# Forget logits in fp32 in the quarters of a bank, and the first bias rows loaded over ScalarE's queue, in a streaming encoder kernel

## The chip, the cores and the metric

The kernel runs on one core of a Trainium2 chip. The time is that of one execution on the device, in microseconds (us). Matrix products run on TensorE (PE in the profile, its weight loads PEld), elementwise work on VectorE (DVE), ScalarE (ACT) and GpSimd (POOL); SyncE (SP) issues DMA transfers, and so can ScalarE and GpSimd, each over a queue of its own.

## The reference

Two layers run over 640 tokens of width 1024: 512 of a prompt and 8 x 16 new ones of samples. Layer 0 mixes with a chunked gMLP. Layer 1, in which the change lies, is forgetting attention with 16 heads of 128 channels. With h the normalized input of the layer:

```
proj = h @ w_in                                  # q, k, v, z (2048 columns each), then 16 forget logits
logf = log_sigmoid(proj[..., 4 * E:] + b_f)      # one number per token and head
cT = cumsum(logf)                                # along the tokens, for each head
s = q @ k.T * dh ** -0.5 + cT[query] - cT[key]   # later keys masked
y = softmax(s) @ v * silu(z), then @ w_out
```

The samples attend in the same way to 256 cached rows and their own new ones. `logf` of all tokens is an output too.

## The kernel before, in words

**Data.** h stands transposed in the tile A as two halves h_hi and h_lo whose sum is h (type fp32r, 8 k-tiles of 128 channels by 640 tokens). A product in full precision is made of several fp32r matmuls over such halves: L272, L273 and L274 are the three of a product. Weights come as units of 512 KB by DMA into RAW or R (for the attention layer GpSimd issues them, L122), GpSimd forms sums of blocks (L211, into sff), and ScalarE (L289) and VectorE (L290) split each unit into two fp32r halves in W. Most projections are made as seven block products in place of eight. For these, `right_operands` (L570) needs the four quarters of whole h, in fp32: (i, j) is half i of the channels by half j of the tokens (320 each). Three were copied by ScalarE when h was made (KEPT, L323); the fourth, (1, 0), is joined from the halves by one VectorE addition, L578.

**Order.** The source lists the work of the projections as steps (`interleave`, L370), and pieces of other work with due times in us are called between the steps. A scheduler that simulates the engines then fixes the order on each engine; every engine works its list in order. `behind` and `queued` pin a piece behind a given instruction.

**The stage.** The attention layer begins with `project_v0` (L1032; matmuls L1040 and L1041), then `project_k0` and `project_q`/`project_z`. Between the steps of `project_v0` stand:

- `forget_logits` (L955): the forget weights, 128 x 8 x 16, are split into two fp32r halves side by side in WF (L932). In two token ranges, 0 to 384 and 384 to 640 (SPLITS), 16 matmuls each (L961, L962, L964) bring w_hi and w_lo times h_hi, and w_hi times h_lo, into 32 and 16 rows of a bank. ScalarE copies them out (L965).
- `log_forget` (L967): five transposes of 32 x 128 (L970), a copy and two additions on VectorE, then log_sigmoid.
- `forget_sums` (L987): the cumulative sums as matmuls with a triangle of ones (L990 for the prompt, L998 to L1000 for the samples). ScalarE copies the results out (L991, L1001) and stores them by DMA: c_sc (16 heads x 512) and cs_sc (the samples' rows, mask of the later scores).

From there on each head needs its bias rows back, spread over 128 partitions: `load_w0(h)` loads row h of c_sc (256 KB; into a slot of sff for even heads, into CST for odd ones), and `load_mask(i)` loads rows of cs_sc (136 KB). For head 0, head 1 and the first mask GpSimd issues these loads (L122, a helper line that names the queue); later ones are issued by ScalarE. VectorE turns a row into the bias of a query block (L1141), and ends the scores of a block with L1151 or L1154, before ScalarE's exponential (L1157) and the normalization (L1162). For the samples it adds a mask to the last 16 columns (L1222), and four matmuls side by side, each writing 32 rows of a bank, make the scores (L1225). L709, L720, L722 and L725 take the block products of the projections out of the banks; L1096 and L1104 are ScalarE's parts of q and z; L317 are transposes of the projections.

## Time and profile before

| | |
|---|---|
| time, median of 3 runs (lowest, highest) | 1284.0 us (1283.24, 1284.87) |
| the profiled execution | 1284.04 us |
| its span | 1281.7 us |
| mean granted TensorE clock | 0.998 |
| busy share: PE, PEld, DVE, ACT, POOL | 99%, 89%, 75%, 46%, 28% |
| chain that ended last: PE, DVE, DMA, issue | 94%, 3%, 2%, 1% |

The span runs from the first to the last instruction. The busy share is that of the whole span, so an engine with 75% can still be the late one in a single stage. A row of a timeline gives start, duration, engine, line, operation, output<-input, shapes and count; where the engine stood idle before it, the brackets give for how long and which engine's result, or which transfer, ended it. A row "PE ... <- DVE ..." of the waits gives the total time that TensorE stood until VectorE's instruction, how often, and the longest. Instructions overlap in the pipeline of TensorE, so what a matmul costs is read from the distance of two starts.

### The profile page before, as it was taken

How to read it: one execution, taken by the hardware profiler on the slowest of the kernel's cores; microseconds unless marked ns; L12 is line 12 of the kernel's file. 1: busy time of each engine (PE TensorE's matmuls, PEld its weight loads, DVE VectorE, ACT ScalarE, POOL GpSimd, SP SyncE). 2: the span in 40 equal slices, each digit the busy share in tenths (PEclk: the TensorE clock that was granted, in tenths of full speed). 3: DMA queues.
4: the chain of work that ended last, by engine and by line, in shares of the span. 5: the costliest groups of instructions: out<-in, count | busy, mean ns of one | idle time of the engine just before them, and what ended most of it. 6: DMA issues, size and time to landing. Idle time of an engine off the chain costs nothing.

```text
span 1281.7 us, 21124 instructions
## 1 busy us (share of the span) xinstructions
PE 1270.6 (99%) x7881; PEld 1141.4 (89%) x7881; DVE 955.7 (75%) x1796; ACT 594.9 (46%) x1075; POOL 360.3 (28%) x326
## 2 busy tenths in 40 slices
PE   9999999999999999998999999999999999999998
PEld 7888999999988888887999999999999999788887
DVE  6844999999944374797987898989897988545643
ACT  5424555444535253554544454545444445445331
POOL 1012444453000010245334545454434430000100
PEclk9999999999999999999999999999999999999999
DMA  5532344232324213548887767677888759632211
GB/s 201 179 99 66 114 122 126 85 98 88 120 95 152 82 50 99 139 105 152 166 168 164 188 162 173 147 179 146 147 160 189 178 106 267 247 128 83 67 62 54
DMA packets 275360, 171.52 MB, mean 134 GB/s; under 512 B 188761, under 2 KB 238601, under 8 KB 275258
## 3 DMA queue, kind: packets, MB, share of 16 engines
q1 hardware_dynamic: 261170, 127.80, 36.5%
q0 software_dynamic: 10000, 36.71, 13.9%
q10 hardware_dynamic: 4088, 5.67, 1.5%
q8 instruction: 62, 1.02, 0.3%
q14 instruction: 40, 0.33, 0.1%
HBM read 148.55 MB, written 21.59 MB: 133 GB/s over the span
## 4 chain that ended last, share of the span: by engine, by line
PE 94%; DVE 3%; DMA 2%; issue 1%; SPq 0%; ACT 0%; POOL 0%; ACTq 0%; DVEq 0%; POOLq 0%
PE pb L272 26%; PE pb L273 26%; PE pb L274 26%; PE pb L1175 3%; PE pb L419 2%; PE pb L1252 2%; PE pb L1168 1%; PE pb L1225 1%; PE pb L317 1%; PE pb L741 1%; DMA out<-R 1%; DVE W L290 1%; PE pb L1040 1%; PE pb L1053 1%; PE pb L1249 1%
## 5 line engine op out<-in xcount | busy, mean ns | idle before, releaser
L272 PE MATMUL pb<-A,W 128*128 128x320 f32 (+1 forms) x752 | 241.4, 321 | 1.9 <-DVE R L720 1.6
L273 PE MATMUL pb<-A,W 128*128 128x320 f32 (+1 forms) x752 | 234.4, 312 | 0.0
L274 PE MATMUL pb<-A,W 128*128 128x320 f32 (+1 forms) x752 | 233.9, 311 | 0.0
L290 DVE TENSOR_TENSOR W<-RAW,W 128x1024 fp32r<-128x1024 f32 (+1 forms) x122 | 148.2, 1215 | 72.5 <-ACT W L289 70.5
L273 PE MATMUL pb<-W,A 128*128 128x512 f32 x498 | 194.6, 391 | 0.0
L272 PE MATMUL pb<-W,A 128*128 128x512 f32 x498 | 194.5, 393 | 0.0
L274 PE MATMUL pb<-W,A 128*128 128x512 f32 x498 | 193.8, 392 | 0.0
L289 ACT ACTIVATE W<-RAW 128x1024 fp32r<-128x1024 f32 (+1 forms) x122 | 115.8, 949 | 91.1 <-PE pb L274 43.4
L272 PEld LDWEIGHTS pb<-A,W 128*128 128x128 f32 x752 | 142.0, 189 | 3.0 <-DVE R L720 1.8
L273 PEld LDWEIGHTS pb<-A,W 128*128 128x128 f32 x752 | 142.1, 189 | 0.6 <-issue 0.2
L274 PEld LDWEIGHTS pb<-A,W 128*128 128x128 f32 x752 | 141.8, 189 | 0.0
L272 PE MATMUL pb<-tbf,W 128*128 128x320 f32 x360 | 118.9, 330 | 0.0
L303 POOL TENSOR_TENSOR SML<-SML 128x1 f32<-128x1 f32 x20 | 14.9, 748 | 351.2 <-DVE SML L301 346.5
L274 PE MATMUL pb<-tbf,W 128*128 128x320 f32 x360 | 111.4, 309 | 0.0
L273 PE MATMUL pb<-tbf,W 128*128 128x320 f32 x360 | 111.2, 309 | 0.0
L274 PEld LDWEIGHTS pb<-W,A 128*128 128x128 f32 x498 | 93.4, 188 | 19.5 <-issue 0.4
L273 PEld LDWEIGHTS pb<-W,A 128*128 128x128 f32 x498 | 93.6, 188 | 18.7
L272 PEld LDWEIGHTS pb<-W,A 128*128 128x128 f32 x498 | 93.5, 188 | 18.6
L211 POOL TENSOR_TENSOR sff<-RAW 128x512 f32<-128x512 f32 x46 | 59.4, 1292 | 178.8 <-DVE W L290 107.6
L709 DVE TENSOR_TENSOR R<-R,pb 128x320 f32<-128x320 f32 x184 | 86.3, 477 | 15.3 <-PE pb L274 13.6
L290 DVE TENSOR_TENSOR A<-R,A 128x640 fp32r<-128x640 f32 (+1 forms) x42 | 34.4, 853 | 56.6 <-ACT A L289 56.2
L272 PEld LDWEIGHTS pb<-tbf,W 128*128 128x128 f32 x360 | 67.7, 188 | 9.8 <-issue 6.2
(280 smaller groups left out, 2860.7 us busy)
## 6 DMA issues: line engine op xcount, KB each, us to landing
RAW<-in_fox_w_in POOLq DMA_DIRECT2D x46, 512.0 KB, 7.4
RAW<-in_gmlp_w_in SPq DMA_DIRECT2D x40, 512.0 KB
R<-in_cache_fox_k SPq DMA_DIRECT2D x128, 128.0 KB
R<-in_cache_fox_v SPq DMA_DIRECT2D x32, 512.0 KB
RAW<-in_gmlp_w_out SPq DMA_DIRECT2D x16, 512.0 KB
RAW<-in_ple_w_gate SPq DMA_DIRECT2D x16, 512.0 KB
RAW<-in_fox_w_out SPq DMA_DIRECT2D x16, 512.0 KB
R<-in_fox_w_in POOLq DMA_DIRECT2D x14, 512.0 KB, 8.1
```

Of the source, the lines that this page charges most:

```text
L211: nc.gpsimd.tensor_tensor(out=o, in0=a, in1=b, op=op)
L272: nc.tensor.matmul(out, lh, rh, start=start, stop=False)
L273: nc.tensor.matmul(out, lh, rl, start=False, stop=False)
L274: nc.tensor.matmul(out, ll, rh, start=False, stop=stop)
L289: first = nc.scalar.activation(out=hi, in_=src, func=AF.Copy)
L290: nc.vector.tensor_tensor(out=lo, in0=src, in1=f(hi), op=ALU.subtract)
L303: behind["pool"] = nc.gpsimd.tensor_tensor(out=q, in0=t, in1=mhalf, op=ALU.pow)
L317: behind["pe"] = nc.tensor.transpose(out=b[:, j * P:(j + 1) * P], in_=src[:, (4 * c + j) * P:(4 * c + j + 1) * P], identity=ident)
L419: line[e] = make(*args, **kw)
L709: behind["dve"] = nc.vector.tensor_tensor(out=into(i, j), in0=a, in1=b, op=ALU.add)
L1175: nc.tensor.matmul(O[:, d], v[:, j, hh * P:(hh + 1) * P], pt[:, j * P:(j + 1) * P], start=(j == 0), stop=(j == i))
L1252: nc.tensor.matmul(O[32 * bl:32 * bl + 32, :256], pt[:, t * P + 32 * bl:t * P + 32 * bl + 32], vv[:, bl, t], start=False, stop=(t == 1))
```

## The change

The forget logits are formed from whole h in fp32. WF becomes fp32 and holds the raw forget weights twice, so that a matmul brings 32 rows of which 16 count twice over. Tokens 0 to 511, four tiles of 128, go into the four quarters (32 rows each) of one bank; tile 2 lies across the two halves of the tokens and takes two matmuls of 64 columns per k-tile. The samples' tile goes into a second bank, with two k-tiles in each quarter, and the four partial sums are added later by one reduction on VectorE. That makes 48 matmuls, two copies on ScalarE and two 128 x 128 transposes. The quarter (1, 0) of h is joined ahead of `project_v0`, since the logits now read it, and `right_operands` takes it as ready. The due times of the pieces in `project_v0` change.

The loads of the rows of heads 0 and 1 and of the first mask are issued by ScalarE, the first of them pinned behind the store of cs_sc.

The diff; new line numbers are some 4 to 18 higher than the old ones (L1141 is L1159 in the new file, L1222 is L1240, L1040 is L1058, L964 and its like become L968):

```diff
@@ -68,7 +68,7 @@
     psum = tc.alloc_tile_pool(name="psum", bufs=1, space=PSUM)
     dram = tc.alloc_tile_pool(name="dram", bufs=1, space=DRAM)
     W = sbuf.tile([P, NW * 2048], F32R, name="W")
-    WF = sbuf.tile([P, 256], F32R, name="WF")
+    WF = sbuf.tile([P, 256], F32, name="WF")
     A = sbuf.tile([P, 10240], F32R, name="A")
     RAW = sbuf.tile([P, NRAW * 1024], F32, name="RAW")
     CST = sbuf.tile([P, C_N], F32, name="CST")
@@ -564,6 +564,11 @@
     def quarter(i, j):
         return tuple(z[:, 4 * i:4 * i + 4, j * HT:(j + 1) * HT] for z in (h_hi, h_lo))
 
+    def joined_quarter(o, i, j):
+        q = r1(o, 1280).rearrange("p (k n) -> p k n", k=4)
+        hi, lo = quarter(i, j)
+        nc.vector.tensor_tensor(out=q, in0=f(hi), in1=f(lo), op=ALU.add)
+
     def right_sum(i):
         return tuple(TB[:, z:z + 4 * HT].rearrange("p (k n) -> p k n", k=4) for z in (i * 2560, i * 2560 + 1280))
 
@@ -574,8 +579,7 @@
         last = t_a if ready else b12
         for q, (i, j) in zip((b11, b12, b21, b22), ((0, 0), (0, 1), (1, 0), (1, 1))):
             if (i, j) not in ready:
-                hi, lo = quarter(i, j)
-                nc.vector.tensor_tensor(out=q, in0=f(hi), in1=f(lo), op=ALU.add)
+                joined_quarter(at[2 * i + j], i, j)
         for o, a, b, dst in ((t_a, b12, b11, 0), (t_b, b22, t_a, 1), (b21, b21, t_b, 2), (last, b22, b12, None)):
             nc.vector.tensor_tensor(out=o, in0=a, in1=b, op=ALU.subtract)
             if dst is not None:
@@ -932,7 +936,8 @@
     wf_raw = tmpa(128).rearrange("p (k n) -> p k n", k=8)
     dma(wf_raw, f_win[0, :, 4 * E:].rearrange("(k p) n -> p k n", p=P))
     wf = WF.rearrange("p (k n) -> p k n", k=8)
-    split(wf[:, :, :H], wf[:, :, H:], wf_raw)
+    for z in (0, H):
+        nc.scalar.activation(out=wf[:, :, z:z + H], in_=wf_raw, func=AF.Copy)
     bfb = tmpa(H)
     dma(bfb, b_f[0].partition_broadcast(P))
     cc = tmpa(256).rearrange("p (t b h) -> p t b h", t=2, b=NB)
@@ -943,8 +948,7 @@
     for t in range(2):
         nc.vector.tensor_copy(out=cr[:, t].rearrange("p (r b h) -> p r b h", r=NB, b=NB), in_=cc[:, t].rearrange("p b (r h) -> p r b h", h=2))
 
-    fT = tmpa(TOK, 32)
-    ft = tmpa(NT * 32).rearrange("p (t c h) -> p t c h", t=NT, c=2)
+    fT = tmpa(2 * P)
     n = NT * H
     fx, fa, fe, fl, fu, lft = (r1(o_V + 1280 + z * n, n) for z in range(6))
     lf3 = lft.rearrange("p (t h) -> p t h", t=NT)
@@ -952,25 +956,37 @@
     cT, ex, cS = r1(o_PT + 288, SEQ, H), r1(o_PT + 800, P), r1(o_V + 1760, 272)
     assert o <= o_K and o_PT + 288 >= o_P + 1280 and o_PTs + 96 >= o_qp + 1280
 
+    def whole(i, j):
+        return r1(KEPT[i, j], 1280).rearrange("p (k n) -> p k n", k=4)
+
     def forget_logits():
-        for (a, b) in SPLITS:
-            pb = bank(ATT)
-            for k in range(8):
-                hi, lo = h_at(k, a, b)
-                if k == 0:
-                    nc.tensor.matmul(pb[:32, :b - a], wf[:, k], hi, start=True, stop=False)
-                nc.tensor.matmul(pb[:H, :b - a], wf[:, k, :H], lo, start=False, stop=False)
-                if k > 0:
-                    nc.tensor.matmul(pb[:32, :b - a], wf[:, k], hi, start=False, stop=(k == 7))
-            nc.scalar.activation(out=fT[:, a:b], in_=pb[:32, :b - a], func=AF.Copy)
+
+        pb = bank(ATT), bank(ATT)
+
+        def add(g, z, t, k, start, stop, j):
+            a, b = max(t * P, j * HT), min((t + 1) * P, (j + 1) * HT)
+            nc.tensor.matmul(pb[z][32 * g:32 * g + 32, a - t * P:b - t * P], wf[:, k], whole(k // 4, j)[:, k % 4, a - j * HT:b - j * HT],
+                             start=start, stop=stop)
+
+        for k in range(8):
+            for t, j in ((0, 0), (1, 0), (3, 1)):
+                add(t, 0, t, k, k == 0, k == 7, j)
+            for n in (2 * k, 2 * k + 1):
+                add(2, 0, 2, n % 8, n % 8 == 0, n % 8 == 7, n // 8)
+        for z in range(2):
+            for g in range(4):
+                add(g, 1, 4, 2 * g + z, z == 0, z == 1, 1)
+        for z in range(2):
+            nc.scalar.activation(out=fT[:, z * P:(z + 1) * P], in_=pb[z][:, :P], func=AF.Copy)
 
     def log_forget():
         pb = bank(ATT)
-        for t in range(NT):
-            nc.tensor.transpose(out=pb[:, t * 32:(t + 1) * 32], in_=fT[:, t * P:(t + 1) * P], identity=ident[:32, :32])
-        nc.vector.tensor_copy(out=ft, in_=pb[:, :NT * 32].rearrange("p (t c h) -> p t c h", t=NT, c=2))
-        nc.vector.tensor_tensor(out=fx3, in0=ft[:, :, 0], in1=ft[:, :, 1], op=ALU.add)
-        nc.vector.tensor_tensor(out=fx3, in0=fx3, in1=bfb.unsqueeze(1).broadcast_to([P, NT, H]), op=ALU.add)
+        for z in (0, P):
+            nc.tensor.transpose(out=pb[:, z:z + P], in_=fT[:, z:z + P], identity=ident)
+        groups = pb[:, :2 * P].rearrange("p (z g h) -> p z g h", z=2, h=32)[:, :, :, :H]
+        nc.vector.tensor_tensor(out=fx3[:, :4], in0=groups[:, 0], in1=bfb.unsqueeze(1).broadcast_to([P, 4, H]), op=ALU.add)
+        nc.vector.tensor_reduce(out=fx3[:, 4], in_=groups[:, 1].rearrange("p g h -> p h g"), op=ALU.add, axis=mybir.AxisListType.X)
+        nc.vector.tensor_tensor(out=fx3[:, 4], in0=fx3[:, 4], in1=bfb, op=ALU.add)
 
         nc.vector.scalar_tensor_tensor(out=fa, in0=fx, scalar=-1.0, in1=fx, op0=ALU.mult, op1=ALU.max)
         nc.scalar.activation(out=fe, in_=fa, func=AF.Exp, scale=-1.0)
@@ -999,7 +1015,9 @@
         nc.tensor.matmul(pb[:, P:272], cr[:, 1], tri[:, :272 - P], start=False, stop=False)
         nc.tensor.matmul(pb[:, 256:272], ex, CST[:, C_T16:C_T16 + TS], start=False, stop=True)
         nc.scalar.activation(out=cS, in_=pb[:, :272], func=AF.Copy)
-        dma(cs_sc, cS, nc.scalar)
+        behind["act"] = nc.scalar.dma_start(out=cs_sc, in_=cS)
+        with queued("act"):
+            load_w0(0, nc.scalar)
 
 
     def v_of(p):
@@ -1323,15 +1341,17 @@
     sums = []
 
     def sums_of_h():
-        sums.append(right_operands((KEPT[0, 0], KEPT[0, 1], o_qp, KEPT[1, 1], o_P), KEPT))
+        sums.append(right_operands((KEPT[0, 0], KEPT[0, 1], KEPT[1, 0], KEPT[1, 1], o_P), KEPT))
 
     def first_k():
         with queued("sp"):
             load_k(0, 0, 0)
 
-    interleave(project_v0(), [(0.0, forget_logits), (2.0, log_forget), (2.1, sums_of_h), (9.0, forget_sums),
-                              (9.1, lambda: load_w0(0, nc.gpsimd)), (1.0, first_k)])
-    interleave(project_k0(), [(11.0, lambda: turn_k(0, 0, 0)), (11.1, lambda: load_k(0, 0, 1)), (0.0, lambda: load_w0(1, nc.gpsimd)), (0.1, lambda: load_mask(0, nc.gpsimd)), (6.0, lambda: load_v(0, 0))])
+    KEPT[1, 0] = o_qp
+    joined_quarter(o_qp, 1, 0)
+    interleave(project_v0(), [(3.0, forget_logits), (4.5, log_forget), (4.6, sums_of_h), (9.0, forget_sums),
+                              (1.0, first_k)])
+    interleave(project_k0(), [(11.0, lambda: turn_k(0, 0, 0)), (11.1, lambda: load_k(0, 0, 1)), (3.0, lambda: load_mask(0, nc.scalar)), (3.1, lambda: load_w0(1, nc.scalar)), (6.0, lambda: load_v(0, 0))])
     split(*quarter(0, 1), sums[0])
     nc.gpsimd.memset(r1(o_qp, 512), 0.0)
     interleave(project_q(0), [(8.0, lambda: turn_k(0, 0, 1)),
```

How the order moves. First TensorE in `project_v0`: pb_70 to pb_73 are the banks of the v projection, pb_74 that of the logits, R_69 the large working tile. This stands on TensorE in the middle of the v projection before:

```order
L1040 MATMUL pb_71<-W,A 128x512
L1041 MATMUL pb_71<-W,A 128x256
L1040 MATMUL pb_71<-W,A 128x512
L317 MATMUL pb_75<-CST,R_69 128x128 x4
L962 MATMUL pb_74<-A,WF 16x384 x2
L964 MATMUL pb_74<-A,WF 32x384
L962 MATMUL pb_74<-A,WF 16x384
L317 MATMUL pb_76<-CST,R_69 128x128 x4
L964 MATMUL pb_74<-A,WF 32x384
```

And this stands on TensorE now, where the large piece of the logits begins, late in the v projection:

```order
L1058 MATMUL pb_73<-W,A 128x512
L968 MATMUL pb_74<-R_69,WF 32x128
L968 MATMUL pb_74<-R_69,WF 32x64 x2
L968 MATMUL pb_74<-R_69,WF 32x128 x3
L968 MATMUL pb_74<-R_69,WF 32x64 x2
L968 MATMUL pb_74<-R_69,WF 32x128 x3
L968 MATMUL pb_74<-R_69,WF 32x64
L317 MATMUL pb_77<-CST,R_69 128x128 x4
L317 MATMUL pb_75<-CST,R_69 128x128 x4
L968 MATMUL pb_74<-R_69,WF 32x64
```

On what moved: part of the old logits lay one or two at a time between other matmuls, the rest in runs; the new ones, each of 64 or 128 columns, stand in four pieces of 2, 13, 25 and 8 matmuls.

Then ScalarE at the end of the cumulative sums: rows with DMA are transfers that it issues. The order on ScalarE before:

```order
L289 ACTIVATE W<-RAW 128x512
L718 ACTIVATE R_69<-pb_71 128x320
L991 ACTIVATE R_69<-pb_74 16x512
L122 DMA c_sc<-R_69 16x512
L289 ACTIVATE W<-sff 128x1024
L1001 ACTIVATE R_69<-pb_75 128x272
L122 DMA cs_sc<-R_69 128x272
```

The order on ScalarE now, at the same place:

```order
L289 ACTIVATE W<-RAW 128x512
L722 ACTIVATE R_69<-pb_71 128x320
L1007 ACTIVATE R_69<-pb_74 16x512
L1017 ACTIVATE R_69<-pb_75 128x272
L122 DMA c_sc<-R_69 16x512
L1018 DMA cs_sc<-R_69 128x272
L289 ACTIVATE W<-sff 128x1024
L122 DMA sff<-c_sc 128x512
L122 DMA CST<-c_sc 128x512
L122 DMA R_69<-cs_sc 128x1x272
```

The three loads of bias rows now stand between the two stores and the next work of ScalarE (L1096, now L1114), with one weight split between the stores and the loads.

And GpSimd at the same place, where these loads stood. The order on GpSimd before:

```order
L122 DMA RAW<-in_fox_w_in 128x4x256 x2
L1205 COPY R_69<-R_69 128x4x16
L122 DMA sff<-c_sc 128x512
L122 DMA CST<-c_sc 128x512
L211 TENSOR_TENSOR sff<-RAW 128x512
L122 DMA R_69<-cs_sc 128x1x272
L211 TENSOR_TENSOR sff<-RAW 128x512
L211 TENSOR_TENSOR sff<-sff,RAW 128x512
L211 TENSOR_TENSOR sff<-RAW,sff 128x512
```

The order on GpSimd now:

```order
L122 DMA RAW<-in_fox_w_in 128x4x256 x2
L1223 COPY R_69<-R_69 128x4x16
L211 TENSOR_TENSOR sff<-RAW 128x512 x2
L211 TENSOR_TENSOR sff<-sff,RAW 128x512
L211 TENSOR_TENSOR sff<-RAW,sff 128x512
L122 DMA RAW<-in_fox_w_in 128x4x256
```

GpSimd keeps its weight loads and sums (L211), without the three loads between them.

## The prediction

> **What bounds the kernel now.** I read the page first, then the waits of TensorE, then the timelines of the engines named there, and last the clock and the DMA share by windows.
>
> ```profile
> span 1281.7 us, 21124 instructions
> ...
> PE 1270.6 (99%) x7881; PEld 1141.4 (89%) x7881; DVE 955.7 (75%) x1796; ACT 594.9 (46%) x1075; POOL 360.3 (28%) x326
> ```
>
> TensorE is busy for 99% of the span. So a change pays in two ways only: TensorE gets less to do, or one of its few stands goes. Of its waits, these three are the ones behind the stage that the change touches:
>
> ```profile
> PE pb L272 <- DVE SML L1154: 2.0, 1, 2.0
> PE pb L272 <- DVE R L720: 1.6, 1, 1.6
> PE pb L272 <- DVE R L725: 0.3, 1, 0.3
> ```
>
> All name VectorE. Its timeline shows why it was late (start, duration, engine, line, operation, and in brackets the idle time before it with its releaser):
>
> ```profile
> 587.06 0.61 DVE L1141 TENSOR_TENSOR R<-sff,CST 128x128 f32<-128x128 f32 x1 [5.64 <-DMA sff<-c_sc]
> 587.60 2.92 DVE L290 TENSOR_TENSOR W<-R,W 128x512 fp32r<-128x512 f32 x2
> 590.44 1.76 DVE L290 TENSOR_TENSOR W<-RAW,W 128x512 fp32r<-128x512 f32 x1
> 592.12 0.47 DVE L720 TENSOR_TENSOR R<-R,pb 128x320 f32<-128x320 f32 x1
> ```
>
> VectorE, which works in order, stood from 581.42 to 587.06 us for the bias rows of head 0. Behind them were queued three weight splits (4.6 us), and behind those L720, whose result TensorE stood 1.6 us for. The stand of 2.0 us at L1154 is ten us later in the same backlog. Then comes the clock (columns: window; its length; busy time and count of PE, PEld, DVE, ACT, POOL; granted clock; DMA share; GB/s):
>
> ```profile
> 572.50:575.50 3.00, 3.00 (x23) 3.00 (x22) 3.00 (x6) 1.35 (x2) 2.92 (x3) 1.00 0.05 11
> 603.80:607.20 3.40, 3.40 (x16) 3.40 (x15) 3.40 (x3) 0.89 (x3) 3.32 (x3) 0.50 0.24 37
> ```
>
> Right behind the stands the clock is granted at 0.50 for 3.4 us: at half speed TensorE loses 1.7 us there. At stake in this place are 2.0 + 1.6 + 0.3 + 1.7 = 5.6 us.
>
> **Why the rows were late.** GpSimd issued them, in its own queue, behind two weight loads of 512 KB:
>
> ```profile
> 575.43 1.52 POOL L122 DMA_DIRECT2D RAW<-in_fox_w_in  x2
> 576.94 0.25 POOL L1205 COPY R<-R 128x64 f32<-128x64 f32 x1
> 577.12 0.56 POOL L122 DMA_DIRECT2D sff<-c_sc  x1
> 577.66 0.55 POOL L122 DMA_DIRECT2D CST<-c_sc  x1
> 578.22 1.31 POOL L211 TENSOR_TENSOR sff<-RAW 128x512 f32<-128x512 f32 x1
> 579.47 0.64 POOL L122 DMA_DIRECT2D R<-cs_sc  x1
> ```
>
> ```profile
> sff<-c_sc POOLq DMA_DIRECT2D x1, 256.0 KB, 9.9
> ```
>
> The first row load took 9.9 us from issue to landing. ScalarE stores what they read, and stands idle around it:
>
> ```profile
> 575.19 0.34 ACTq L122 DMA_DIRECT2D cs_sc<-R  x1
> 577.41 0.31 ACT L1096 ACTIVATE R<-R 128x128 f32<-128x128 f32 x1 [2.26 <-DVE R L709]
> 577.63 1.04 ACT L289 ACTIVATE W<-sff 128x1024 fp32r<-128x1024 f32 x1
> 579.52 0.31 ACT L1096 ACTIVATE R<-R 128x128 f32<-128x128 f32 x1 [0.84 <-DVE R L709]
> 581.05 1.58 ACT L289 ACTIVATE W<-R 128x512 fp32r<-128x512 f32 x2 [1.22 <-DVE R L709]
> 583.51 0.63 ACT L289 ACTIVATE W<-RAW 128x512 fp32r<-128x512 f32 x1 [0.88 <-DMA RAW<-in_fox_w_in]
> ```
>
> **The change part by part.** *Forget logits removed.* The second bank of the old form reads:
>
> ```profile
> 549.30 0.28 PE L1041 MATMUL pb<-W,A 128*128 128x256 f32 x1
> 549.41 0.28 PE L961 MATMUL pb<-A,WF 128*32 128x256 f32 x1
> 549.53 0.39 PE L962 MATMUL pb<-A,WF 128*16 128x256 f32 x2
> ...
> 551.24 0.40 PE L1040 MATMUL pb<-W,A 128*128 128x512 f32 x1
> ```
>
> ```profile
> 537.78 0.33 PE L964 MATMUL pb<-A,WF 128*32 128x384 f32 x1
> 537.95 0.40 PE L1040 MATMUL pb<-W,A 128*128 128x512 f32 x1
> ```
>
> Sixteen matmuls of 256 columns took 551.24 - 549.41 = 1.8 us; those of 384 columns go by every 0.17 us, so sixteen are 2.8 us. Of the transposes:
>
> ```profile
> 542.44 1.09 PE L317 MATMUL pb<-CST,R 128*128 128x128 f32 x8
> 543.46 0.31 PE L970 MATMUL pb<-CST,R 32*128 32x32 f32 x2
> 543.70 0.50 PE L1040 MATMUL pb<-W,A 128*128 128x512 f32 x1
> ```
>
> Two 32-column transposes took 543.70 - 543.46 = 0.24 us, and five some 0.7 with their breaks. Removed: 1.8 + 2.8 + 0.7 = 5.3 us.
>
> *Forget logits added.* 640 tokens in 8 k-tiles are 5120 columns, 1280 in each quarter of a bank, in 48 fp32 matmuls. Two rows bound them. The first is the sample scores, which also lay four matmuls side by side in quarters; the second is the cumulative sum, fp32 matmuls one after another:
>
> ```profile
> 585.84 1.12 PE L1225 MATMUL pb<-R 128*32 128x272 f32 x16
> 586.89 0.42 PE L272 MATMUL pb<-tbf,W 128*128 128x320 f32 x1
> ```
>
> ```profile
> 569.00 2.33 PE L990 MATMUL pb<-CST,R 128*16 128x512 f32 x8
> 571.26 0.41 PE L273 MATMUL pb<-A,W 128*128 128x320 f32 x1
> ```
>
> An fp32 matmul leaves two records. Side by side, 544 columns per quarter took 1.05 us, 1.93 ns a column, so 1280 cost 2.5 us. One after another, 1280 columns took 2.26 us, so 5120 cost 9.0. A count in place of columns gives 1.05 / 8 = 0.13 us a matmul, and 48 of them 6.3. I take 2.5, because the L1225 row is the same kind of work: 32 output rows, four quarters in turn. Two 128x128 transposes cost 2 x (543.46 - 542.44) / 8 = 0.26. The new order lays the logits in four pieces between other matmuls; for three more breaks I estimate 3 x (0.28 - 0.11) = 0.5, the 0.28 us one matmul lasts less the 0.11 it takes in the stream. Added: 3.3; net **-2.0 us**, with ends of -2.5 (no breaks) and +4.5 (one after another).
>
> One rule speaks against this. Going from whole-array matmuls to quarters and back, the rows above show no gap: 549.30, 549.41, 549.53 are spaced like the rest of the stream. The Trainium skill, TensorEngine Tiling (Array Packing), section Tiling Modes, says of changes of the tiling mode that "Mode switching requires drain"; by that rule the sum of this part would come out smaller, and as no row shows the drain, I leave it to the rivals.
>
> *Row loads moved.* In the new order the three loads (648 KB together) stand on ScalarE's queue right behind the two stores and one split, so they issue at about 577 at the latest on the old time scale, when the stores have landed, ahead of no large transfer of their own queue. The DMA engines had a share of 0.05 at 572.5 to 575.5, so there is room. VectorE asks for the rows at 581.42, over 4 us later. The L1141 stand (5.64) should go, and with it the stands of 1.6 and 0.3 us. What is late next is the weight unit for which ScalarE waited 0.88 us at 583.51, and the scores at L1154: VectorE's work ahead of them partly waits for TensorE's banks, so it doesn't all move up by 5.64. I keep 1.6 us of the 5.6 for that, and take **-4.0 us**. The ends are 1.9 (only 1.6 + 0.3 go, the rest and the clock stay) and 5.6 (all goes); 4.0 lies nearer to the upper one, because the half clock follows directly on the stands.
>
> *New waits.* On ScalarE the loads wait for the landing of the stores; L1096 and the splits of L289 are queued behind. GpSimd issued its load of c_sc at 577.12 and that of cs_sc at 579.47 without a wait in the row, so the second store, issued at 575.19, had landed within 4.3 us. At worst ScalarE is 2.1 us late at 577.41, and its waits of 0.84 + 1.22 + 0.88 = 2.9 us after it take that up: nothing. On VectorE the mask's addition (L1222) now stands right behind L1141 and ahead of the splits and L720; it needs the third load, which lands last. If that comes after 582, VectorE stands again, with L720 behind it: this is in the 1.6 us kept. *The rest at nothing:* the two copies that replace the split of the forget weights, the early join of a quarter of h (the same VectorE addition), fewer copies on ScalarE, two small reductions on VectorE: none is among TensorE's waits, since v projections fill TensorE there. If the join (about as long as a split) came late, the logits would only slide behind it in the stream. GpSimd loses three DMA issues.
>
> *Sum:* 1284.04 (the profiled run, 1281.7 of span and 2.34 outside; the median is 1284.0) - 2.0 - 4.0 = **1278.0 us**.
>
> **The rivals.** *The loads gain nothing.* Rows land no earlier, or another transfer takes their place: 1284.04 - 2.0 = 1282.0 us. For it: at 577 the two weight loads are under way, and 648 KB share the engines with them. Against it: the share of 0.05 before, and that the rows' 9.9 us were spent behind 1 MB of their own queue. The Trainium skill, DMA: Bandwidth & Descriptors, section Issuing engines are not separate DMA queues, says that loads of all issuing engines end on the same 16 engines, so another issuer saves only the issuing time. No run here has yet shown such a load from ScalarE at this place.
>
> *A drain at each change of tiling.* Four pieces are eight changes; with a gap of 0.28 - 0.11 = 0.17 us at each, 1.4 us: the first part is worth -0.6, and the time is 1279.4. The Trainium skill's rule above (TensorEngine Tiling) is this one; the rows at 549.41 speak against it.
>
> *Quarters one after another.* The first part costs +4.5: 1284.04 + 4.5 - 4.0 = 1284.5 us. The L1225 rows speak against it. This is also the case in which the change doesn't do what its words say.
>
> *All stands go:* 1284.04 - 2.0 - 5.6 = 1276.4 us.
>
> *Slower: ScalarE stands for its stores.* If the second store takes as long as a queued load did, 9.9 us, it lands at 585.1; ScalarE's work of 577.41 is 7.7 us late, less the 2.9 us of idle time 4.8, and TensorE stands for the weights that are split there. The rows, issued after it, land no earlier than before, so the old 5.6 us stay: 1284.04 - 2.0 + 4.8 = 1286.8 us. It decides once the store lands later than 577.41 + 2.9 = 580.3. The bound of 4.3 us above speaks against it; the tighter traffic speaks for it.
>
> **How the numbers follow.** The forecast, a part of the stands gone, has 0.60; all stands gone 0.10; a drain 0.07; loads that gain nothing 0.13; quarters one after another 0.05; ScalarE's stand 0.05. 0.2% (about what a measurement of this kernel can tell from no change) is 2.6 us: faster means under 1281.4, slower over 1286.6. Faster: 0.60 + 0.10 + 0.07 = 0.77; same: 0.13 + 0.05 = 0.18; slower 0.05. The range reaches from both cheap ends together, 1284.04 - 2.5 - 5.6 = 1275.9, less the 0.8 us by which runs of before lay off their median, 1275.1, to the case in which the loads gain nothing, 1282.0; serial quarters and ScalarE's stand, 0.10, are left out.
>
> **What would show it.** Right: VectorE's wait at L1141's place under 1 us; the three load rows on ScalarE's queue landing within 5 us; no wait of 1.6 us for L720; the clock at 1.00 where it was 0.50; all logits matmuls in about 3 us of TensorE's stream. Wrong: VectorE standing 2 us or more for the mask's row; ScalarE standing at the load's issue with L289 late; weights landing so much later that TensorE stands for their splits; a logits stretch of 6 us or more; or the half clock moved to another place.

## The result and the profile after

The changed kernel takes 1275.76 us (median of 6 runs, 1274.95 to 1276.05), the kernel before 1284.79 in the same comparison (6 runs). The ratio is 0.9934, with a 95% interval from 0.9925 to 0.9944: 7 to 10 us less. The profiled execution took 1274.95 us, 9.1 less than that of before.

The page of the changed kernel, its first lines and the chain that ended last:

```profile
span 1273.1 us, 21241 instructions
...
PE 1265.6 (99%) x7942; PEld 1138.3 (89%) x7942; DVE 957.5 (75%) x1795; ACT 595.3 (47%) x1076; POOL 353.3 (28%) x323
...
PE 98%; DVE 2%; DMA 0%; issue 0%; ACT 0%
```

The waits of TensorE over the whole program. The three rows of before (2.0, 1.6 and 0.3 us) are gone. One small wait is new in this stage, the one for L1099, at 571.63 us. The row of L726 lies at 161.72 us, far ahead of the change, and before has its like there (L722, 0.3 us in two waits):

```profile
PE pb L401 <- DVE r2a_t L393: 1.5, 1, 1.5
PE pb L410 <- DVE r2a_t L419: 0.4, 1, 0.4
PE pb L272 <- DVE R L1099: 0.4, 1, 0.4
PE pb L272 <- DVE R L726: 0.2, 1, 0.2
```

VectorE at the bias rows: the row's addition (L1159, L1141 before) waits for nothing, the mask's (L1240, L1222 before) 0.23 us, and L724 (L720 before) starts at 583.02 in place of 592.12. The mask, issued at 572.09 (below), is not there before 580.45:

```profile
579.95 0.28 DVE L1159 TENSOR_TENSOR R<-sff,CST 128x128 f32<-128x128 f32 x1
580.45 0.18 DVE L1240 TENSOR_TENSOR R<-R,CST 128x16 f32<-128x16 f32 x1 [0.23 <-DMA R<-cs_sc]
580.55 1.96 DVE L290 TENSOR_TENSOR W<-R,W 128x512 fp32r<-128x512 f32 x2
582.42 0.69 DVE L290 TENSOR_TENSOR W<-RAW,W 128x512 fp32r<-128x512 f32 x1
583.02 0.48 DVE L724 TENSOR_TENSOR R<-R,pb 128x320 f32<-128x320 f32 x1
```

ScalarE's queue, with the two stores and the three loads:

```profile
569.21 0.34 ACTq L122 DMA_DIRECT2D c_sc<-R  x1
569.65 0.38 ACTq L1018 DMA_DIRECT2D cs_sc<-R  x1
570.89 1.06 ACT L289 ACTIVATE W<-sff 128x1024 fp32r<-128x1024 f32 x1 [1.43 <-PE pb L273]
571.24 0.33 ACTq L122 DMA_DIRECT2D sff<-c_sc  x1
571.61 0.44 ACTq L122 DMA_DIRECT2D CST<-c_sc  x1
572.09 1.17 ACTq L122 DMA_DIRECT2D R<-cs_sc  x1
```

In before, GpSimd's two weight loads went out at 575.43, ahead of the rows. Now they come behind the two rows:

```profile
572.33 1.51 POOL L122 DMA_DIRECT2D RAW<-in_fox_w_in  x2
```

The logits on TensorE, the two large pieces and what follows each:

```profile
539.85 0.84 PE L968 MATMUL pb<-R,WF 128*32 128x128 f32 x24
540.62 1.09 PE L317 MATMUL pb<-CST,R 128*128 128x128 f32 x8
541.65 1.42 PE L968 MATMUL pb<-R,WF 128*32 128x64 f32 x52
542.99 0.39 PE L1059 MATMUL pb<-W,A 128*128 128x256 f32 x1
```

Where the time went is read by putting the same matmul of both timelines of TensorE side by side:

| matmul | before | after | difference | step |
|---|---|---|---|---|
| ahead of the logits (L317) | 527.27 | 526.57 | -0.70 | |
| behind them (L358) | 557.29 | 554.66 | -2.63 | -1.93 |
| L274 | 575.11 | 573.34 | -1.77 | +0.86 |
| sample scores (L1225, now L1243) | 585.84 | 584.08 | -1.76 | +0.01 |
| behind the first stand (L273) | 592.90 | 589.25 | -3.65 | -1.89 |
| behind the second (L273) | 603.02 | 596.48 | -6.54 | -2.89 |
| values (L1252, now L1270), half clock before | 607.71 | 599.64 | -8.07 | -1.53 |
| L273 | 1048.14 | 1039.71 | -8.43 | -0.36 |
| L272 | 1099.10 | 1090.14 | -8.96 | -0.53 |

The first 0.70 us arise ahead of the change, within the first 50 us; this offset differs from one execution to the next (from -0.7 to +1.4 in the traces of the experiments), so it is no effect of the change. The logits give 1.93. Then 0.86 is lost: 0.66 at the wait for L1099 (0.39 of stand and a slow restart behind it), and 0.2 among the matmuls of the cumulative sums, which now lie in another order. The stands, the half clock and the small wait at L1168 behind it give 1.89 + 2.89 + 1.53 + 0.36 = 6.7. The last 0.53 arise at 1064 us, where TensorE stood 0.28 us for ScalarE's L1170 before and does not now; why was not followed up.

### The profile page after: what moved, and what is told of

It is laid out like the page before. It is cut to its first block, busy times and chain, and to the rows that moved or that the text cites. A ratio compares the mean times of both kernels' runs of the same rounds, so it can differ in the third digit from the quotient of the medians.

```text
span 1273.1 us, 21241 instructions
## 1 busy us (share of the span) xinstructions
PE 1265.6 (99%) x7942; PEld 1138.3 (89%) x7942; DVE 957.5 (75%) x1795; ACT 595.3 (47%) x1076; POOL 353.3 (28%) x323
## 3 DMA queue, kind: packets, MB, share of 16 engines
q8 instruction: 62, 1.02, 0.3%
## 4 chain that ended last, share of the span: by engine, by line
PE 98%; DVE 2%; DMA 0%; issue 0%; ACT 0%
PE pb L272 27%; PE pb L274 27%; PE pb L273 27%; PE pb L1193 3%; PE pb L419 2%; PE pb L1270 2%; PE pb L1186 1%; PE pb L1243 1%; PE pb L745 1%; PE pb L317 1%; PE pb L1058 1%; PE pb L1071 1%; PE pb L1267 1%; DVE W L290 0%; PE pb L1262 0%; PE pb L1059 0%
## 5 line engine op out<-in xcount | busy, mean ns | idle before, releaser
L272 PE MATMUL pb<-A,W 128*128 128x320 f32 (+1 forms) x752 | 240.8, 320 | 0.0
L273 PE MATMUL pb<-A,W 128*128 128x320 f32 (+1 forms) x752 | 233.8, 311 | 0.0
L274 PE MATMUL pb<-A,W 128*128 128x320 f32 (+1 forms) x752 | 233.3, 310 | 0.0
L273 PE MATMUL pb<-W,A 128*128 128x512 f32 x498 | 194.6, 391 | 0.0
L272 PE MATMUL pb<-W,A 128*128 128x512 f32 x498 | 194.6, 393 | 0.0
L274 PE MATMUL pb<-W,A 128*128 128x512 f32 x498 | 193.8, 392 | 0.0
L272 PEld LDWEIGHTS pb<-A,W 128*128 128x128 f32 x752 | 141.7, 188 | 1.0 <-issue 0.2
L273 PEld LDWEIGHTS pb<-A,W 128*128 128x128 f32 x752 | 141.7, 188 | 0.5
L274 PEld LDWEIGHTS pb<-A,W 128*128 128x128 f32 x752 | 141.2, 188 | 0.0
L272 PE MATMUL pb<-tbf,W 128*128 128x320 f32 x360 | 119.0, 330 | 0.4 <-DVE R L1099 0.4
L274 PE MATMUL pb<-tbf,W 128*128 128x320 f32 x360 | 111.4, 309 | 0.0
L273 PE MATMUL pb<-tbf,W 128*128 128x320 f32 x360 | 111.2, 309 | 0.0
L274 PEld LDWEIGHTS pb<-W,A 128*128 128x128 f32 x498 | 93.4, 188 | 19.3 <-issue 0.4
L273 PEld LDWEIGHTS pb<-W,A 128*128 128x128 f32 x498 | 93.6, 188 | 18.8
L272 PEld LDWEIGHTS pb<-W,A 128*128 128x128 f32 x498 | 93.5, 188 | 18.6
L211 POOL TENSOR_TENSOR sff<-RAW 128x512 f32<-128x512 f32 x46 | 60.9, 1324 | 177.4 <-DVE W L290 114.6
L272 PEld LDWEIGHTS pb<-tbf,W 128*128 128x128 f32 x360 | 67.8, 188 | 10.4 <-issue 6.6
```

What stands on the lines that cost most here:

```text
L211: nc.gpsimd.tensor_tensor(out=o, in0=a, in1=b, op=op)
L272: nc.tensor.matmul(out, lh, rh, start=start, stop=False)
L273: nc.tensor.matmul(out, lh, rl, start=False, stop=False)
L274: nc.tensor.matmul(out, ll, rh, start=False, stop=stop)
```

## The experiments

All times are medians against the kernel before, run on the same chip; ratios carry their 95% intervals. In the edits "before" and "after" name the two kernels. The first question was which of the two parts gives the gain. **Theory Q** (the forecast's) held that GpSimd's queue made the rows late, **rival S** that the earlier stores make them early.

**loads_only**: before, with the three loads moved to ScalarE.

```diff
-        dma(cs_sc, cS, nc.scalar)
+        behind["act"] = nc.scalar.dma_start(out=cs_sc, in_=cS)
+        with queued("act"):
+            load_w0(0, nc.scalar)
...
-(9.1, lambda: load_w0(0, nc.gpsimd))
...
-(0.0, lambda: load_w0(1, nc.gpsimd)), (0.1, lambda: load_mask(0, nc.gpsimd))
+(3.0, lambda: load_mask(0, nc.scalar)), (3.1, lambda: load_w0(1, nc.scalar))
```

> The kernel before, with the three loads of bias rows on ScalarE's queue and the old forget logits. Theory Q (the rows were late because they lay in GpSimd's queue behind two weight loads of 512 KB, and all the stands with the half clock follow from that): VectorE's stand of 5.64 us at L1141 falls under 1 us, and the time to about 1278.5 us (1277.5 to 1280), that is 6 us under the kernel before. Rival S (the rows come early in the changed kernel because the new logits let the sums be stored some 4 us sooner): with the old logits the stores are as late as before, VectorE stands 2 us or more for the rows or the mask, and the time is 1281 to 1283.

Measured: 1286.58 us, ratio 1.0013 (1.0004 to 1.0022). That is above both ranges: the loads alone gain nothing; they cost a little. Its timelines of ScalarE, SyncE and VectorE show where the loads stay:

```profile
576.83 0.39 ACTq L122 DMA_DIRECT2D sff<-c_sc  x1
580.26 0.33 ACTq L122 DMA_DIRECT2D CST<-c_sc  x1
580.63 0.31 ACT L1098 ACTIVATE R<-R 128x128 f32<-128x128 f32 x1 [4.27 <-DMA sff<-c_sc]
587.97 1.17 ACTq L122 DMA_DIRECT2D R<-cs_sc  x1
589.19 0.31 ACT L1098 ACTIVATE R<-R 128x128 f32<-128x128 f32 x1 [7.30 <-issue]
```

```profile
576.71 9.64 SPq L124 DMA_DIRECT2D out<-R  x8
```

```profile
591.71 0.17 DVE L1224 TENSOR_TENSOR R<-R,CST 128x16 f32<-128x16 f32 x1 [7.56 <-DMA R<-cs_sc]
```

ScalarE stands 4.3 and 7.3 us around the issue of the second and third load, while SyncE's eight stores of k are being issued (a row with x8 holds all eight). VectorE now stands for the mask (L1224), 7.6 us, with three splits and L720 behind it. And ScalarE's late copies of q (L1098) reach TensorE. The row names GpSimd, but L211 had been done long before; L1098 ends at 589.50, and the sample scores start at 589.60:

```profile
589.60 1.20 PE L1227 MATMUL pb<-R 128*32 128x272 f32 x16 [2.49 <-POOL sff L211]
```

The Trainium skill, DMA: Bandwidth & Descriptors, section Issuing engines are not separate DMA queues, says that the issuing engine saves only issuing time. For this run the measurement agrees: another queue for these three loads, with nothing else changed, is worth nothing.

**logits_only**: after, with the three loads given back to `nc.gpsimd` at the due times of before.

> The changed kernel with the three loads back on GpSimd's queue. Theory Q: GpSimd issues them behind the two weight loads, VectorE stands 4 us or more at the same place, the clock is granted at half behind it, and only the logits' gain is left: 1282 to 1284 us. Rival S: with the earlier stores the rows come early on any queue, and the time is 1276 to 1278.

Measured: 1280.24 us, ratio 0.9967 (0.9955 to 0.998), about -4.2 us. Between the two: VectorE still stands for the row, but 3.3 us in place of 5.6.

```profile
585.06 0.50 DVE L1157 TENSOR_TENSOR R<-sff,CST 128x128 f32<-128x128 f32 x1 [3.26 <-DMA sff<-c_sc]
```

TensorE's first stand (1.6 us, L720) is gone, the second (2.0) and the half clock stay, and one of 1.7 us (at L1184) is new. Both Q and S fall as they were put: the parts alone give -4.2 and +1.7 us, together -8.5. Six of the 8.5 us come only from both together.

**serial**: after, with the same 48 matmuls issued quarter after quarter.

```diff
-        for k in range(8):
-            for t, j in ((0, 0), (1, 0), (3, 1)):
+        for t, j in ((0, 0), (1, 0), (3, 1)):
+            for k in range(8):
                 add(t, 0, t, k, k == 0, k == 7, j)
...
```

> The changed kernel with the same 48 logits matmuls, issued quarter after quarter: all k-tiles of one token tile before the next. If matmuls of different quarters run side by side and those of one quarter one after another (1.8 us for 1280 columns, as in the cumulative sum's rows), the logits take 7 to 9 us of TensorE in place of 3.1 and the time is 1279.5 to 1282. If each fp32 matmul costs its issue and not its columns, the order does not matter: 1275.8.

Measured: 1286.11 us, ratio 1.0005 (0.9996 to 1.0014). Its two large pieces:

```profile
539.48 2.65 PE L968 MATMUL pb<-R,WF 128*32 128x128 f32 x30
542.06 1.09 PE L317 MATMUL pb<-CST,R 128*128 128x128 f32 x8
543.08 2.66 PE L968 MATMUL pb<-R,WF 128*32 128x128 f32 x42
545.67 0.39 PE L1059 MATMUL pb<-W,A 128*128 128x256 f32 x1
```

They take 2.58 and 2.59 us for 15 and 21 matmuls, against 0.77 and 1.34 for 13 and 25 in the changed kernel. With the two small pieces the logits take 6.75 us, against 3.02 in turn: matmuls of different quarters do run side by side. On TensorE's timeline this step costs 3.8 us. The 6.75 us are a little less than the 7 to 9 expected, and yet the time lies above the expected range, 10.3 us over the changed kernel's median (9 by the ratios). The rest comes behind the logits: the stores and loads are later, TensorE stands 3.3 us at L1172, and the clock is at half for 6.8 us (3.4 in before, none in the changed kernel). Delaying the logits by 3.8 us loses the whole gain of the change. (The 1.8 us in the expectation should read 1.8 ns a column: the rows of the cumulative sum give 2.26 us for 1280 columns.)

**mask_gpsimd**: after, with only the mask's load back on GpSimd.

> The changed kernel with only the load of the first mask back on GpSimd's queue; the two rows of c_sc stay with ScalarE. The mask's addition stands on VectorE right behind L1159 (L1141 before) and ahead of three splits. Theory Q: the mask lands some 9 us after its issue at about 574, at 583; VectorE stands 2 to 4 us there for it, and the time is 1278 to 1281. If the mask's place does not matter: 1275.8 as in the changed kernel.

Measured: 1282.06 us, ratio 0.9978 (0.9967 to 0.9989). The mask alone takes back most of the gain.

```profile
585.48 1.17 DVE L1240 TENSOR_TENSOR R<-R,CST 128x16 f32<-128x16 f32 x1 [3.43 <-DMA R<-cs_sc]
```

The mask is issued at 575.05, behind GpSimd's two weight loads, and takes 10.4 us to land. The stand was foreseen, the time lies 1 us above the expected range, and the queue as the reason was not yet settled. So the next runs asked what holds the loads: **theory H** says SyncE's stores, **rival C** the weights on the same DMA engines.

**no_stores**: loads_only without `store_k` for the second head of `project_k0`.

> The run with the loads alone moved to ScalarE (loads_only), without SyncE's eight stores of the second k head: that part of the key output is left out. Theory H: in loads_only ScalarE stood 3.4 and 7.3 us at the issue of the second and third load, because each had to wait for one of these small-packet stores that were in flight on SyncE's queue just before it; without them ScalarE stands under 1 us there, the sample scores no longer make TensorE stand for 2.5 us, and the time is 1277 to 1281 us. Rival C (the loads were slowed by the weight loads that share the DMA engines, not by the stores): ScalarE still stands 5 us or more, and the time stays above 1283.

Part of the key output is missing in this run, so its time only tells of the loads. Measured: 1284.41 us, ratio 0.9996 (0.9987 to 1.0004). Half of H holds, the half that matters does not:

```profile
575.12 0.39 ACTq L122 DMA_DIRECT2D sff<-c_sc  x1
575.55 0.46 ACTq L122 DMA_DIRECT2D CST<-c_sc  x1
576.64 1.17 ACTq L122 DMA_DIRECT2D R<-cs_sc  x1
```

```profile
587.88 1.22 DVE L1225 TENSOR_TENSOR R<-R,CST 128x16 f32<-128x16 f32 x1 [7.19 <-DMA R<-cs_sc]
```

ScalarE no longer stands at the issue, so the stores did hold it. But the mask, issued at 576.64, still lands 11 us later, and VectorE stands 7.2 us as before. Issue in time is not landing in time.

**row_only**: before, with only `load_w0(0)` on ScalarE, behind the store of cs_sc.

> The kernel before, with only the row of head 0 loaded over ScalarE's queue; head 1's row and the mask stay on GpSimd's, the logits are the old ones. Theory H: this load is issued ahead of the stores' hold, so ScalarE does not stand; VectorE gets its row by 580, does not stand 5.6 us at L1141, and if the mask's addition lies behind L720 as before, the time is 1279 to 1282; if VectorE stands for the mask instead, 1282 to 1285. Rival C: the row lands no earlier than 586, 1284.

Measured: 1281.25 us, ratio 0.9972 (0.9959 to 0.9984), with a wide spread (1277.8 to 1286.0). The row, issued at 575.59, is there when VectorE asks at 581.30. It goes out 1.5 us earlier than in before (577.12), together with GpSimd's weight loads (from 575.40) and not behind them. So with the old logits one row on ScalarE's queue gains some 3.6 us, where all three loads gained nothing. Here the mask's addition lies behind the splits but ahead of L720; VectorE stands 3.8 us for it there, and the time is still that of the range without this stand.

**late_loads**: after, with the three loads pinned behind the copy of q on ScalarE.

> The changed kernel with the three loads pinned on ScalarE's queue behind the copies of q (L1114 there), some 6 us later than in the changed kernel; the logits are the new ones. Theory H (the queue alone does not help: the loads must go out before SyncE's stores and early enough for VectorE, which the shorter logits make possible): ScalarE or VectorE stands 3 us or more for them, the clock is granted at half for 3.4 us, and the time is 1280 to 1286. Rival Q (ScalarE's queue by itself makes the rows early): 1275.5 to 1277.5.

Measured: 1280.81 us, ratio 0.9964 (0.9952 to 0.9976). The first load goes out at 582.13, and VectorE stands 5.7 us for its row. The size is as expected, but the clock is not granted at half: TensorE's longest stand is 1.85 us. With the new logits in place, ScalarE's queue does not keep the gain when the loads go out late: the time is that of GpSimd's queue (logits_only, 1280.24). The two runs do not compare the queues at the same moment. Measured from the start of the stage, the first row is issued 7.9 us later here and is there 2.4 us later.

**mask_add_later**, **loads_add_later**, **after_add_later**: mask_gpsimd, loads_only and after, each with one VectorE instruction moved, the mask's addition, to behind the first prompt scores.

```diff
-            with queued("dve"):
+            with queued("mask" if p == 0 and bg == 0 else "dve"):
                 nc.vector.tensor_tensor(out=Wc[:, PAST:]
```

> The run with the mask's load on GpSimd's queue (mask_gpsimd, where VectorE stood 3.4 us for the mask and the time was 1282), with one instruction moved on VectorE: the addition of the mask now follows the first prompt scores (L1172) in place of the row's addition (L1159), so the three splits and L724 no longer lie behind it. Theory V (VectorE, working in order, stands for whichever row lands last, and the splits and L724 behind it make TensorE stand and the clock fall): VectorE's wait for the mask falls under 1 us, the clock stays at 1.00, and the time is 1275.5 to 1277.5. Rival W (the late mask holds the sample scores, or the 136 KB slow the weights, wherever the addition lies): 1280 to 1282.5.

> The run with the loads alone moved and the old logits (loads_only, 1286.6), with the same one instruction moved. Theory V with two causes: VectorE's stand of 7.6 us for the mask goes, but ScalarE still stands at the issue of the second and third load behind SyncE's stores, so its copy of q (L1098) is late and TensorE still stands 2.5 us for the sample scores, with the half clock behind it: 1282 to 1285. If VectorE's stand alone is the cost: 1277 to 1279.

> The changed kernel with the same one instruction moved. There VectorE stands only 0.23 us for the mask. Theory V: nothing to gain, 1275.3 to 1276.2; if VectorE's addition ahead of the splits costs more than its wait, down to 1275.0.

Measured: 1284.09 us (ratio 0.9993, 0.9984 to 1.0003), 1284.99 (1.0005, 0.9996 to 1.0013) and 1276.82 (0.9941, 0.9927 to 0.9955). Theory V fails in the first: VectorE's wait for the mask falls to 0.85 us as it said, but the time does not. The next transfer takes its place, the loads of cached keys on SyncE:

```profile
586.37 1.08 DVE L1242 TENSOR_TENSOR R<-R,CST 128x16 f32<-128x16 f32 x1 [0.85 <-DMA R<-cs_sc]
...
600.29 1.42 DVE L1221 STREAM_TRANSPOSE R<-R 128x256 f32<-128x256 f32 x4 [6.22 <-DMA R<-in_cache_fox_k]
```

TensorE then stands 5.9 us. The time is above Rival W's range too. In the second run ScalarE's stands remain, as expected; the 1.6 us by which its median lies under loads_only are 1.0 by the ratios, whose intervals overlap, so a gain is not shown. In the third there was nothing to gain. So moving this one instruction on VectorE does not free the stage. A common bound that is left is the DMA, which the next run looks at.

**rows_sync**: after, with the three loads on SyncE's queue. Nothing moves on the other engines. **Theory D**: what counts is that the 648 KB go out while the DMA engines are idle.

```diff
-            load_w0(0, nc.scalar)
+            load_w0(0, nc.sync)
...
-(3.0, lambda: load_mask(0, nc.scalar)), (3.1, lambda: load_w0(1, nc.scalar))
+(3.0, lambda: load_mask(0, nc.sync)), (3.1, lambda: load_w0(1, nc.sync))
```

> The changed kernel with the three loads on SyncE's queue in place of ScalarE's; nothing else moves on the other engines. There the two rows stand behind one store of k, and the mask behind three more. Theory D (what counts is that the 648 KB go out in the 3 us in which the DMA engines are idle, before the weight loads, the k stores and the k loads fill them; the queue only decides when a load is issued): the mask is issued 4 us or more later than in the changed kernel, VectorE stands 2 us or more for it, the k loads come later too, and the time is 1278.5 to 1283. Rival Q (a hardware queue of its own, other than GpSimd's, is enough): VectorE stands under 1 us, 1275.5 to 1277.

Measured: 1281.08 us, ratio 0.9966 (0.9954 to 0.9978). As D said. SyncE issues the rows behind a store:

```profile
575.05 0.33 SPq L124 DMA_DIRECT2D out<-R  x1
575.49 1.35 SPq L122 DMA_DIRECT2D sff<-c_sc  x1
576.92 1.32 SPq L122 DMA_DIRECT2D CST<-c_sc  x1
578.29 2.50 SPq L124 DMA_DIRECT2D out<-R  x3
580.89 0.70 SPq L122 DMA_DIRECT2D R<-cs_sc  x1
```

VectorE stands 2.7 us for the row and 1.5 for the mask, TensorE 2.0, and the clock is at half for 3.4 us. The first row goes out 4.3 us later than in the changed kernel and the mask 8.8 us later (0.9 us of both is the offset of this trace). The next four rows are 3 us windows of the changed kernel, of before, of loads_only and of rows_sync, in this order, each around the start of GpSimd's two weight loads (issued from 572.33, 575.43, 576.63 and 573.26). They show the idle stretch and whether it was used (the last two columns are the DMA share and GB/s):

```profile
571.24:574.24 3.00, 2.61 (x18) 2.61 (x19) 3.00 (x6) 0.71 (x1) 2.84 (x4) 1.00 0.46 147
```

```profile
573.00:576.00 3.00, 3.00 (x23) 3.00 (x23) 3.00 (x5) 1.35 (x2) 2.92 (x3) 1.00 0.01 3
```

```profile
574.20:577.20 3.00, 3.00 (x23) 3.00 (x23) 3.00 (x5) 1.34 (x2) 2.92 (x3) 1.00 0.10 21
```

```profile
572.20:575.20 3.00, 2.63 (x18) 2.64 (x19) 3.00 (x5) 0.69 (x1) 2.82 (x4) 1.00 0.18 26
```

At 147 GB/s for 3 us the changed kernel has moved some 0.44 MB by then, rows and the first of the weights together; before has moved next to nothing. Some 3 us later the DMA engines are full in both, the changed kernel first and before second:

```profile
577.00:580.00 3.00, 3.00 (x23) 3.00 (x22) 3.00 (x8) 0.94 (x3) 0.00 (x0) 1.00 1.00 173
```

```profile
577.00:580.00 3.00, 3.00 (x23) 3.00 (x22) 3.00 (x8) 1.57 (x3) 2.98 (x5) 1.00 0.94 131
```

A row that goes out from there on should share the engines with the weights; the windows do not say whose bytes they moved.

**quarter_later**: after, with the split of quarter (0, 1) of h pinned behind L1099, against the wait for L1099.

> The changed kernel with the split of quarter (0, 1) of h placed behind the k channels' last addition on VectorE (L1099), to take away the new stands of 0.4 and 0.2 us there, where the trace of the changed kernel loses 0.9 us against the one before. If VectorE's two long splits ahead of L1099 are the cause: those stands go and the time is 1274.5 to 1275.5; as the split of h moves too, TensorE may stand for it instead, 1276 to 1279.

Measured: 1277.08 us, ratio 0.994 (0.9929 to 0.9952). The wait for L1099 is gone from TensorE's list (that for L726, far ahead of this stage, is not), but a stand of 1.3 us at L1186 has come. The time is in the second of the expected ranges. No version here beats the changed kernel.

## Why the prediction was right

The forecast was 1278.0 us, the median is 1275.76, near the lower end of the range.

**The logits: right.** The forecast was -2.0 us with 3.3 us added; the timeline shows -1.93, and 3.02 us for the four pieces (0.34 + 0.77 + 1.34 + 0.57) plus 0.2 for the transposes. The L1225 rows were the right model. Issued quarter after quarter they take 6.75 us, where the forecast's other end was 9.0 and its count 6.3.

**A drain at each change of tiling.** The Trainium skill's rule (TensorEngine Tiling (Array Packing), section Tiling Modes) asks for one. The large piece starts at 539.85, where the 512-column matmul ahead of it, from 539.53, would end its 0.23 us share of the stream at 539.76: a gap of 0.09 us. On the way back, the transposes behind it (L317) take 1.03 us, as they did before (1.02). So there may be something, but at these two changes less than the 0.17 that the rival set for each of eight, and the forecast's 0.5 us for breaks covers it.

**The waits: right in direction and kind, too small in size.** The forecast was -4.0, with 5.6 at most. The stands and the clock gave 6.7, and 0.86 was lost again, so -5.8 remain. The forecast kept 1.6 us back for what would be late next; of that only 0.86 came, and at another place (the wait for L1099 and the sums' new order, not the weights or the scores; with the split that lies ahead of L1099 on VectorE moved, in quarter_later, that wait is gone). The stands removed also cost more than the three rows that were summed: the steps of the table hold besides a stand the slow restart behind it (0.25 us in place of 0.15 from 592.65 to the next matmul) and a small wait (0.17 at L1168).

**The step that failed: why the loads come early.** The forecast let them issue "at about 577 at the latest on the old time scale" and took the room for them from a window at 572.5 to 575.5, where the DMA share was 0.05. Those two do not fit together. With the old logits the first load goes out at 575.6 on that scale (575.59 in row_only; 576.83 in loads_only, whose trace is 1.2 us later from the start on), when the idle stretch ends. That row is still in time, the mask behind it is not, and the three together gain nothing. It was the new logits and the new order that came with them, not the queue, that brought all three into the stretch: the second store goes out at 569.65 in place of 575.19, 5.5 us earlier. Of this 0.7 is the offset from the start and 1.9 TensorE's shorter work. The rest, some 2.9, is order. On TensorE the last matmuls of the sums (L1016, L1000 before) stand one matmul behind the large ones in place of eleven, which is 1.5 us. On ScalarE the second copy of the sums now stands ahead of the split that used to wait 1.85 us for GpSimd. So the forecast added two terms that mostly hang on each other; that it came out near, because both parts were made at once, is in part luck. Row_only shows that the queue is not worth nothing by itself: there one row gains 3.6 us with the old logits.

One of its signs of being right also failed: the three loads were to land within 5 us. The mask took some 8 (572.09 to 580.45), against 9.3 before. What the change moved is when the loads go out, much more than how long they take.

**The rivals.** The one of 1282.0 ("the loads gain nothing") and the slower one ("ScalarE stands", 1286.8) describe the loads without the new logits well: 1286.58, with ScalarE standing 7.3 us. They were wrong for the change because the loads were issued (571.24 to 573.26) before SyncE's stores (from 574.12). The forecast's reason for the slower one, a late landing of ScalarE's own store, was not the one seen: no_stores shows that SyncE's stores hold the issue. How they hold it was not tried by itself. The wait of the mask's addition on VectorE, named as a new wait, is the one that most variants meet (3.4 us in mask_gpsimd), and the changed kernel passes it with 0.23 us.

**Open.** VectorE stands 6.2 us for the loads of cached keys in mask_add_later and not at all in mask_gpsimd, though SyncE issues them at the same moment of the stage (587.97 and 587.19, traces that are 0.8 us apart from the start on) and the only difference is one addition on VectorE. Why they land later was not found. That the moment of issue decides is shown by late_loads and rows_sync, which keep the new logits and lose 4 to 5 us. That a late load is slow because the DMA engines are full is supported by the windows, but no run took the weights away.

## What to carry to other kernels

Before pricing an earlier load, look at the DMA share in the window in which it will really be issued, not in the one before it; here loads that just missed an idle stretch landed with the traffic that ended it. Two edits can be worth more together than their sum: ask of each what the other must have done by then, and test each alone. And when a stand is removed, look for the next transfer in the same full stretch: in mask_add_later it was the next stand.

## What the runs showed of the hardware

**Stands of about 2 us of TensorE came with a clock at half for 3.4 us.** In the 13 profiles read for this (all but after_add_later), every kernel with a stand of 2.00 us or more between 589 and 607 us (before, rows_sync, mask_gpsimd, logits_only with 2.00; loads_add_later 2.18; row_only 2.33; no_stores 2.46; loads_only 2.49; serial 3.34; mask_add_later 5.86) has a stretch of half clock there, of 3.4 us or, in the last two, 6.8, where it begins during the stand. Half the clock for 3.4 us is a loss of 1.7 us, an estimate that the step of 1.53 of the table bears out. The three without one had at most 0.4 (after), 1.33 (quarter_later) and 1.85 (late_loads). The length of a stand alone does not decide, though. In logits_only the clock stays at 1.00 from the end of the 2.00 stand (600.65) to 606.40, and the half clock comes right behind a later stand of 1.71; stands of 1.7 us in loads_only, loads_add_later, no_stores and row_only were followed by none. What decides was not tried. In rows_sync and late_loads:

```profile
601.10:604.50 3.40, 3.40 (x13) 2.85 (x12) 3.40 (x4) 0.84 (x3) 3.32 (x4) 0.50 0.14 22
```

```profile
598.00:612.00 14.00, 11.44 (x80) 9.72 (x81) 13.26 (x29) 6.98 (x17) 7.43 (x6) 1.00 0.74 122
```

The Trainium skill, TensorE: Matmul & The Clock Gate, Part 1, gives a window of about 3.4 us after which the clock changes, and says that it falls after an idle window of that length. The length of the stretches agrees; the condition does not, since stands of 1.71 to 2.49 us were enough here.

**fp32 matmuls of 32 output rows run side by side** when they are issued to the quarters in turn: 48 of them took 3.02 us, and 6.75, 2.2 times as long, one quarter after another, with nothing else changed in the source.

**A DMA issue can hold its engine.** ScalarE stood 7.3 us at an issue while another engine's eight stores were being issued (loads_only), and not when these were left out (no_stores).
